# The last pair's sums, splits and stores written into the second feed-forward product's first unit, and a difference tile moved onto their memory

## The chip, the cores and the metric

The kernel runs on one core of one Trainium2 chip. The metric is the device time of one execution in microseconds. The core's engines work side by side, each through a queue of its own in a fixed order: PE multiplies matrices into accumulator banks, DVE and ACT do elementwise work (ACT also the conversions), SP issues the transfers between device memory and on-chip memory, POOL does almost nothing here.

## The reference

One layer of a hybrid trunk on 512 tokens of width 2048: a modulated norm, a projection that feeds a gated linear recurrence and a stick-breaking attention, an output projection, and then the part that this text is about, the gated feed-forward block:

```python
h = rms_norm(x, norm2_g[layer]) * (1.0 + sc2) + sh2
gate, up = jnp.split(h @ w_ffn_in[layer], 2, axis=-1)
x = x + g2 * ((jax.nn.silu(gate) * up) @ w_ffn_out[layer])
```

The inner width is 5632, which is 44 blocks of 128.

## The kernel before, in words

Every matrix product is made of three float products: each operand is split into a rounded part ("hi", a conversion on ACT, L231 or L1101) and the rest ("lo", a subtraction on DVE, L232 or L1102), and hi·hi, hi·lo and lo·hi are added up in the accumulator. Both feed-forward products also use a Strassen-like scheme with seven half-size products in place of eight. So operands have to be added and subtracted before they are split, and results have to be copied out of the accumulators and added up.

**First product.** A loop over f = 2 to 43 takes one pair of 128-wide gate and up blocks each. It loads two weight tiles (`wg`, `wu`), forms sums and differences of their halves on DVE (`ffS` L1133, then L1134 to L1136), splits them, and runs the seven products in the order 1, 2, 6, 7, 5, 4, 3, each 24 matmuls, into the accumulators `ffA`, `ffB` and `ffC`. In between ACT copies partial results out ("taps" a, b, c, u, L1027). DVE and ACT then make silu(gate)·up: the "act", 128 rows by 512 tokens.

`keep` puts the acts of two neighbouring f into one tile `forms` (L1081 for the even f, L1083 for the odd). The seven operand forms of the second product are sums of its quarters (`sums`, L1089 to L1093). `parts` then splits them, a range of forms at a time, and sends both halves to device memory, to be loaded again by the second product:

```python
S.copy(hi, R[:, q])                                               # L1101
V.tensor_sub(R[:, q].bitcast(F32R), R[:, q], hi.bitcast(F32))     # L1102
for i, t in enumerate((hi.bitcast(F32), R[:, q])):
    nc.sync.dma_start(opd[c][:, q, n - starts[c], i * HT:i * HT + HT], t)   # L1104
```

These five steps of a pair (two of `sums`, three of `parts`: forms 0 to 2, 3 and 4, 5 and 6) go into a list `later`, and `one_later()` takes one off after each product of the next f. The last pair has no next f, so `while later: one_later()` (L1169) takes its five steps between the two products. Its hi parts lie in `cond`, an older tile that the second product also uses for copies.

**Second product.** It runs in twelve units `u`, (chunk c of inner blocks) × (column half i); the first four units hold three blocks, the others four. In each unit the seven products run in the order 2, 1, 7, 6, 4, 5, 3 into accumulator pairs `foB`, `foA`, `foC`, `foA`, `foC`, `foA`, `foA`; `multiply` splits two weight blocks at a time (`wfo_<product>_<first block>`, and every fourth pair in a spare place that the profile calls `opsB`) and issues the matmuls. Weight differences are formed in place, and one of them, y3 − y0, in a tile `T2` of its own (in unit 0 in a slice of `yraw`). After product 1 the two `foA` banks are copied by `onto` (L1217 in the first two units, otherwise L1222 with an add) to the output tile `O`. Product 6 goes on adding in the same two banks, so it cannot begin before these copies have read them:

```python
def onto(dst, src, first):
    if first:
        with tc.high_priority(offset=2 * AHEAD):
            S.copy(dst, src)                                      # L1217
        return
```

**What sets the order.** The instructions are written in program order, and a scheduler of the framework puts them into a fixed order per engine, by priorities (`tc.high_priority` lifts a step), data dependencies and the reuse of memory. Tiles come from pools; `rp` holds `forms`, `tp` the other temporaries of the first product, and the second product's pool `zp` (`T2`, `ident2`, `O`) takes over their memory when both are closed (`tctx.close()`, L1171).

Of the kernel before, what the change touches and what calls it, by code (L numbers as in the profile page):

```python
# [10 lines left out]
F32 = mybir.dt.float32  # L11
# [6 lines left out]
P = 128  # L18
D = 2048
KT = 16  # L20
T = 512
# [5 lines left out]
CHUNKS = (3, 3, 4, 4, 4, 4)  # L27
# [102 lines left out]
def trunk(ctx, tc, a):  # L130
# [862 lines left out]
    later = hp.tile([P, 2, HALF, 2, HT], F32R, tag="hlo", name="opC")  # L993
    H.update({6: late[:, 0], 7: late[:, 1], 5: later[:, 0], 4: later[:, 1]})
    for j in range(HALF):
        V.tensor_sub(block(0, 0, j), block(0, 1, j), block(0, 0, j))
        t2 = ft.tile([P, HT], F32, tag="t", name=f"t2_{j}")
# [11 lines left out]
    xctx.close()  # L1009

    tctx = ctx.enter_context(ExitStack())
    tp = tctx.enter_context(tc.tile_pool(name="tp", bufs=2, side="right", reuse_waits="tile"))
    rp = tctx.enter_context(tc.tile_pool(name="rp", bufs=1, side="right", reuse_waits="tile"))
    opd = [dram.tile([P, 7, n, 2 * HT], F32, name=f"opd{c}") for c, n in enumerate(CHUNKS)]
    starts = [sum(CHUNKS[:c]) for c in range(len(CHUNKS))]

# [16 lines left out]
    def place(n):  # L1033
        n %= 11
        return places[0][:, n] if n < 4 else places[1][:, n - 4] if n < 7 else places[2][:, n - 7]

    def load_op(c, q):
        if c < len(CHUNKS):
            nc.sync.dma_start(place(7 * c + q)[:, 0:CHUNKS[c]].bitcast(F32),
                              opd[c][:, ORDER[q] - 1].rearrange("p n (h t) -> p n h t", h=2))  # L1040

    def load_y(u, b):
        if u == len(units):
            return
        c, i = units[u]
        n = CHUNKS[c]
        t = raw_tile([P, n, T], f"wfo{u}_{b}") if b % 2 == 0 else yraw[u > 0][:, b // 2, 0:n]
        nc.sync.dma_start(t, a["w_fo"][i, b][:, starts[c]:starts[c] + n])
        blocks[u][b] = t

    yraw = []
# [21 lines left out]
    forms = {}  # L1073
# [34 lines left out]
    later = []  # L1108

    def one_later():  # L1110
        if later:
            later.pop(0)()
# [13 lines left out]
    for f in range(2, FM):  # L1126
# [39 lines left out]
            keep(f, sg, up)  # L1166
        if rest:
            rest.pop(0)()
    while later:  # L1169
        one_later()  # L1170
    tctx.close()  # L1171


# [8 lines left out]


    zp = ctx.enter_context(tc.tile_pool(name="zp", bufs=1, side="right", reuse_waits="tile"))
    T2 = zp.tile([P, 4, T], F32, name="T2")
    ident2 = zp.tile([P, 512], F32, name="ident2")[:, 0:P]
    O = zp.tile([P, 4, D], F32, name="O")
    A = [att(f"foA{j}") for j in range(2)]
# [6 lines left out]
    def multiply(out, c, q, raw, first, u, sums):  # L1195
        n = CHUNKS[c]
        x = place(7 * c + q)
        for k0 in range(0, n, 2):
            w = min(2, n - k0)
            with tc.high_priority(offset=AHEAD):  # L1200
                for d, e, g in sums:
                    V.tensor_sub(*(t[:, k0:k0 + w] for t in (d, e, g)))
            whi, wlo = split(raw[:, k0:k0 + w], [P, w, T], f"wfo{u}_{q}_{k0}")
            for j in range(2):
                js = slice(j * P, j * P + P)
                for kk in range(w):
                    k = k0 + kk
                    flags = dict(stop=False, skip_group_check=True)
                    PE.matmul(out[j], x[:, k, 0, js], whi[:, kk], start=first and k == 0, **flags)
                    PE.matmul(out[j], x[:, k, 0, js], wlo[:, kk], start=False, **flags)  # L1210
                    flags["stop"] = k == n - 1
                    PE.matmul(out[j], x[:, k, 1, js], whi[:, kk], start=False, **flags)
# [6 lines that stand above are left out]
        t = cond[:, taps[0] % 4 * T:taps[0] % 4 * T + T]  # L1219
        taps[0] += 1  # L1220
        with tc.high_priority(offset=2 * AHEAD):
            S.copy(t, src)  # L1222
        V.tensor_add(dst, dst, t)
# [14 lines left out]
    def some_out(n):  # L1238
        for _ in range(min(n, len(outs))):
            emit_out(*outs.pop(0))  # L1240

    for u, (c, i) in enumerate(units):
        def dst(th, j, dh):
            return O[:, 2 * th + j, dh * 1024 + i * T:dh * 1024 + i * T + T]

        def ready(th, dh):
            if c == last_c:
                outs.extend((8 * dh + 4 * i + m, th) for m in range(4))

        first, final = c == 0, c == last_c  # L1250
        if final and i == 0:
            for g in range(4):
                nc.sync.dma_start(place(7 * c + 7 + g).bitcast(F32).rearrange("p n h t -> p n (h t)"), x1d[:, 4 * g:4 * g + 4])
        if u == 2:
            nc.sync.dma_start(ident2, a["cst"][:, 0])
        y = blocks[u]
        t2 = (T2 if u else yraw[0][:, 2])[:, 0:CHUNKS[c]]
        load_y(u + 1, 2)
        load_y(u + 1, 0)
        for q, p in enumerate(ORDER):  # L1260
            out = {2: B[i], 7: C, 4: C}.get(p, A)
            raw = {2: y[2], 1: y[0], 7: y[1], 6: t2, 4: y[2], 5: y[0], 3: y[3]}[p]
            sums = {7: [(y[1], y[3], y[1])], 6: [(t2, y[3], y[0])], 4: [(y[2], y[2], t2)]}.get(p, ())
            if p == 7:
                with tc.high_priority(offset=AHEAD):
                    for k0 in range(0, CHUNKS[c], 2):
                        ks = slice(k0, min(k0 + 2, CHUNKS[c]))
                        V.tensor_sub(y[0][:, ks], y[1][:, ks], y[0][:, ks])
            multiply(out, c, q, raw, p in (1, 7) or p == 2 and first, u, sums)
            if final:  # L1270
                some_out(3)
            for j in range(2):
                if p == 1:
                    onto(dst(0, j, 0), A[j], first)
                    if final:
                        V.tensor_add(dst(0, j, 0), B[i][j], dst(0, j, 0))
                elif p == 7:
                    onto(dst(1, j, 1), C[j], first)
                elif p == 6:
                    onto(dst(1, j, 0), A[j], first)  # L1280
                elif p == 4:
                    V.tensor_add(dst(1, j, 0), C[j], dst(1, j, 0))
                elif p == 5:
                    onto(dst(1, j, 1), A[j], False)
                elif p == 3:
                    if first:
                        S.copy(dst(0, j, 1), A[j])
                    else:
                        V.tensor_add(dst(0, j, 1), A[j], dst(0, j, 1))
            if p == 1:  # L1290
                ready(0, 0)
                if final:
                    slots += [t[:, h * HT:h * HT + HT] for t in B[i] for h in range(2)]
            elif p in (4, 5, 3):
                ready(*{4: (1, 0), 5: (1, 1), 3: (0, 1)}[p])
            if p == 7:
                load_y(u + 1, 1)
            if p == 3:
                load_y(u + 1, 3)
            if u == 0 and q == 6:  # L1300
                places.append(hp.tile([P, 4, 4, 2, HT], F32R, tag="hhi", name="opsC"))
            if q < 4 and i == (c == 0):
                load_op(c + 1, q)
            if i == 1 and 1 <= q < 4:
                load_op(c + 1, q + 3)
# [60 lines left out]
```

## Time and profile before

| | us |
|---|---|
| median of the three runs | 2292.98 |
| lowest, highest run | 2292.85, 2294.41 |
| the profiled execution | 2288.73 |
| its span, first to last instruction | 2286.7 |

The span has the first product's loop from about 1003 to 1837 us and the second product from there to the end. Rows of a timeline give the start in us, the duration of the row in us, engine, line, operation, names (out <- in), shape and count; in square brackets stands the idle time of the engine before the row and who ended it. Where a row stands for several instructions (x18), its duration runs to the modelled end of the last one; the next row's start says when the engine went on.

### The profile page before, as it was taken

The page shows a single profiled execution, that of the slowest core. Times are in us where ns is not written, and L with a number is a line of the kernel's source. Part 1 is how long each engine was busy: PE and PEld are TensorE (multiplying, and loading weights), DVE is VectorE, ACT ScalarE, POOL GpSimd, SP SyncE. Part 2 cuts the span into 40 slices and gives each one's busy share as a digit, 9 for nine tenths or more (in the row PEclk, how much of TensorE's full clock was granted, in tenths as well). Part 3 has the DMA queues.
Part 4 walks back from the last instruction along what each step waited for, and adds up shares of the span by engine and source line. Part 5 has one row for each costly group of instructions (what it writes and reads, how often), then busy time and mean ns, then how long its engine had stood idle before and what let it go on. Part 6 is the DMA issues. An engine that isn't in the chain of part 4 may idle for free.

```text
span 2286.7 us, 35537 instructions
## 1 busy us (share of the span) xinstructions
PE 2228.2 (97%) x14171; PEld 2025.8 (89%) x14171; DVE 1915.4 (84%) x2566; ACT 1156.0 (51%) x2015; POOL 10.0 (0%) x25
## 2 busy tenths in 40 slices
PE   7999899999999999999999999999999999999999
PEld 6899899878888878899999999999999977778787
DVE  8887779899887865599999888888888878888888
ACT  4326666566655522565454545455555445544443
POOL 0000000000000000000000000000000000000000
PEclk9999999999999999999999999999999999999999
DMA  9886546853332386346555644444444586666452
GB/s 369 314 326 220 174 145 228 303 188 111 112 110 74 111 310 228 97 143 226 185 208 198 225 149 169 150 153 166 132 171 143 178 310 225 238 221 221 151 199 75
DMA packets 114977, 437.68 MB, mean 191 GB/s; under 512 B 9822, under 2 KB 58236, under 8 KB 76796
## 3 DMA queue, kind: packets, MB, share of 16 engines
q1 hardware_dynamic: 114812, 435.42, 53.1%
q8 instruction: 111, 1.82, 0.3%
q14 instruction: 54, 0.44, 0.1%
HBM read 386.61 MB, written 48.77 MB: 190 GB/s over the span
## 4 chain that ended last, share of the span: by engine, by line
PE 64%; DVE 20%; DMA 7%; issue 5%; ACT 3%; SPq 0%; DVEq 0%; ACTq 0%
PE ffA L93 10%; PE foA L93 9%; PE wo L93 7%; PE sbp L93 7%; PE ffC L93 5%; PE foC L93 4%; PE st L93 4%; PE hgf L93 3%; PE hgg L93 3%; PE hgq L93 3%; DVE ff L232 3%; DMA opd<-fhi 2%; PE ffB L93 2%; PE ff L93 2%; DVE ada L179 1%
## 5 line engine op out<-in xcount | busy, mean ns | idle before, releaser
L93 PE MATMUL sbp<-wsb,hhi 128*128 128x384 f32 x1024 | 269.8, 343 | 3.1 <-DVE wsb L232 1.7
L179 DVE SCALAR_TENSOR_TENSOR ada<-ada,cond 128x2048 f32<-128x2048 f32 x95 | 217.0, 2289 | 48.1 <-DMA ada<-in_w_ada 47.9
L93 PEld LDWEIGHTS sbp<-wsb,hhi 128*128 128x128 f32 x1024 | 185.2, 190 | 7.9 <-issue 3.3
L93 PE MATMUL sbp<-wsb,hlo 128*128 128x384 f32 x512 | 172.9, 338 | 0.0
L93 PE MATMUL wo<-ohi,wo 128*128 128x512 f32 x480 | 150.2, 392 | 4.1 <-ACT wo L231 1.6
L232 DVE TENSOR_TENSOR wfo<-wfo,wfo 128x1024 fp32r<-128x1024 f32 (+1 forms) x72 | 83.3, 1164 | 39.7 <-ACT wfo L231 39.3
L93 PEld LDWEIGHTS wo<-ohi,wo 128*128 128x128 f32 x480 | 89.7, 188 | 24.3 <-ACT wo L231 2.9
L93 PE MATMUL ffA<-opD,ff 128*128 128x256 f32 x768 | 99.0, 286 | 4.0 <-ACT u L1027 4.0
L231 ACT CAST wfo<-wfo 128x1024 fp32r<-128x1024 f32 (+1 forms) x72 | 72.2, 1007 | 60.1 <-PE foA L93 56.9
L93 PE MATMUL ffC<-opC,ff 128*128 128x256 f32 x768 | 94.7, 279 | 5.8 <-ACT c L1027 5.8
L93 PEld LDWEIGHTS ffA<-opD,ff 128*128 128x128 f32 x768 | 95.6, 194 | 4.5 <-ACT u L1027 4.5
L1101 ACT CAST fhi<-forms 128x512 fp32r<-128x512 f32 (+1 forms) x63 | 43.7, 693 | 109.3 <-DMA opd<-fhi 76.2
L93 PEld LDWEIGHTS sbp<-wsb,hlo 128*128 128x128 f32 x512 | 97.0, 190 | 0.8 <-issue 0.5
L93 PEld LDWEIGHTS ffC<-opC,ff 128*128 128x128 f32 x768 | 90.8, 188 | 7.2 <-ACT c L1027 7.2
L93 PE MATMUL ffA<-opB,ff 128*128 128x256 f32 x768 | 93.3, 277 | 1.7 <-ACT ff L231 1.0
L93 PE MATMUL wo<-olo,wo 128*128 128x512 f32 x240 | 93.5, 390 | 0.1
L93 PE MATMUL ffB<-opA,ff 128*128 128x256 f32 x768 | 92.7, 276 | 0.0
L93 PEld LDWEIGHTS ffA<-opB,ff 128*128 128x128 f32 x768 | 90.1, 188 | 2.2 <-ACT ff L231 1.2
L93 PE MATMUL ffA<-opA,ff 128*128 128x256 f32 x744 | 89.9, 276 | 0.8 <-DVE ff L232 0.8
L93 PE MATMUL ffA<-opC,ff 128*128 128x256 f32 x744 | 90.1, 277 | 0.0
L93 PEld LDWEIGHTS ffB<-opA,ff 128*128 128x128 f32 x768 | 89.8, 188 | 0.0
L93 PE MATMUL ffC<-opB,ff 128*128 128x256 f32 x744 | 89.7, 276 | 0.0
(1008 smaller groups left out, 5955.5 us busy)
## 6 DMA issues: line engine op xcount, KB each, us to landing
ada<-in_w_ada SPq DMA_DIRECT2D x95, 1024.0 KB, 5.2
wfo<-in_w_fo SPq DMA_DIRECT2D x16, 1024.0 KB, 5.7
yraw<-in_w_fo SPq DMA_DIRECT2D x16, 1024.0 KB, 4.9
fix<-in_w_fix SPq DMA_DIRECT2D x14, 1024.0 KB, 5.5
opd<-forms SPq DMA_DIRECT2D x44, 256.0 KB, 4.7
opd<-fhi SPq DMA_DIRECT2D x42, 256.0 KB, 4.4
opsC<-opd SPq DMA_DIRECT2D x10, 1024.0 KB, 4.8
opsA<-opd SPq DMA_DIRECT2D x9, 1024.0 KB, 7.0
```

The lines of the kernel that those rows point to most:

```text
L93: self.engine.matmul(out, lhsT, rhs, **kw)
L179: V.scalar_tensor_tensor(w, w, 1.0, row, op0=ALU.mult, op1=ALU.mult, accum_out=col)
L231: S.copy(hi, r)
L232: V.tensor_sub(lo, r, hi.bitcast(F32))
L1101: S.copy(hi, R[:, q])
```

## The change

Three things are edited. The steps of the last pair are no longer taken in a row between the products; unit 0 of the second product takes two of them after its second product (q = 1, product 1), two after the third (product 7) and one after the fourth (product 6). For that the tile `forms` has to live on: its pool `rp` is opened ahead of `tp` and stays open. And `T2` is no longer a tile of `zp`, but the next tile of the tag `forms` in `rp`, allocated at u = 1, so that it lies where the forms of the last pair lay.

```diff
     tctx = ctx.enter_context(ExitStack())
+    rp = ctx.enter_context(tc.tile_pool(name="rp", bufs=1, side="right", reuse_waits="tile"))
     tp = tctx.enter_context(tc.tile_pool(name="tp", bufs=2, side="right", reuse_waits="tile"))
-    rp = tctx.enter_context(tc.tile_pool(name="rp", bufs=1, side="right", reuse_waits="tile"))
...
         if rest:
             rest.pop(0)()
-    while later:
-        one_later()
     tctx.close()
...
     zp = ctx.enter_context(tc.tile_pool(name="zp", bufs=1, side="right", reuse_waits="tile"))
-    T2 = zp.tile([P, 4, T], F32, name="T2")
+    T2 = []
...
         y = blocks[u]
-        t2 = (T2 if u else yraw[0][:, 2])[:, 0:CHUNKS[c]]
+        if u == 1:
+            T2.append(rp.tile([P, 4, T], F32, tag="forms", name="T2", bufs=1))
+        t2 = (T2[0] if u else yraw[0][:, 2])[:, 0:CHUNKS[c]]
...
             elif p in (4, 5, 3):
                 ready(*{4: (1, 0), 5: (1, 1), 3: (0, 1)}[p])
+            for _ in range({1: 2, 2: 2, 3: 1}.get(q, 0) if u == 0 else 0):
+                one_later()
             if p == 7:
                 load_y(u + 1, 1)
```

The built programs show where the scheduler puts the instructions. The first place is ACT in unit 0, from the conversion for product 6's first two weight blocks (`wfo_3_0`) on. `CAST cond<-forms` are the last pair's conversions, `COPY O<-foA` the two copies after product 1, `COPY O<-foC` those after product 7; the numbers behind a name are allocation numbers and differ between the builds. Before:

```order
L231 CAST wfo_3_0_18442<-yraw_18316 128x1024
L231 CAST opsB<-yraw_18316 128x512
L231 CAST wfo_3_2_18458<-yraw_18316 128x512
L231 CAST wfo_4_0_18470<-wfo_2_18311 128x1024
L1101 CAST cond<-forms_18089 128x512
L231 CAST opsB<-wfo_2_18311 128x512
L1101 CAST cond<-forms_18089 128x512
L1101 CAST cond<-forms_18089 128x768
L1217 COPY O<-foA_18351 128x512
L1217 COPY O<-foA_18352 128x512
L1217 COPY O<-foC 128x512 x2
```

The same place with the change:

```order
L231 CAST wfo_3_0_18436<-yraw_18316 128x1024
L1215 COPY O<-foA_18333 128x512
L1215 COPY O<-foA_18334 128x512
L231 CAST opsB<-yraw_18316 128x512
L231 CAST wfo_3_2_18452<-yraw_18316 128x512
L231 CAST wfo_4_0_18468<-wfo_2_18311 128x1024
L1101 CAST cond<-forms_18089 128x512
L1215 COPY O<-foC 128x512 x2
L231 CAST opsB<-wfo_2_18311 128x512
L1101 CAST cond<-forms_18089 128x768
L1101 CAST cond<-forms_18089 128x512
```

The conversions of the last pair stood in unit 0 already; what moved is the copies of `foA`, from behind seven conversions to the place right behind `wfo_3_0`, and with them the copies of `foC`.

The second place is DVE in the same stretch, where the lo parts are made and the forms summed (`L1202`/`L1200`: weight differences). Before:

```order
L1202 TENSOR_TENSOR wfo_2_18311<-wfo_2_18311,yraw_18316 128x1024
L232 TENSOR_TENSOR opsB<-yraw_18316,opsB 128x512
L232 TENSOR_TENSOR wfo_3_0_18442<-yraw_18316,wfo_3_0_18442 128x1024
L232 TENSOR_TENSOR wfo_3_2_18458<-yraw_18316,wfo_3_2_18458 128x512
L1202 TENSOR_TENSOR wfo_2_18311<-wfo_2_18311,yraw_18316 128x512
L1089 TENSOR_TENSOR forms_18089<-forms_18089 128x256
```

With the change:

```order
L1200 TENSOR_TENSOR wfo_2_18311<-wfo_2_18311,yraw_18316 128x1024
L232 TENSOR_TENSOR wfo_3_0_18436<-yraw_18316,wfo_3_0_18436 128x1024
L232 TENSOR_TENSOR opsB<-yraw_18316,opsB 128x512
L232 TENSOR_TENSOR wfo_3_2_18452<-yraw_18316,wfo_3_2_18452 128x512
L1200 TENSOR_TENSOR wfo_2_18311<-wfo_2_18311,yraw_18316 128x512
L1089 TENSOR_TENSOR forms_18089<-forms_18089 128x256
```

The lo part of product 7's third block (`opsB<-yraw`) now stands behind that of product 6's first two (`wfo_3_0`).

The third place is DVE at the start of the first product's loop, f = 2, where the two pools' exchanged places in memory change what a first write waits for. Before:

```order
L1081 TENSOR_TENSOR forms_8651<-held 128x2x256
L1133 TENSOR_TENSOR ffS_8658<-wu2r 128x1024
L1083 TENSOR_TENSOR forms_8651<-held 128x2x256
L1134 TENSOR_TENSOR wu2r<-wg2r,wu2r 128x1024
L1089 TENSOR_TENSOR forms_8651<-forms_8651 128x256
L1135 TENSOR_TENSOR wg2r<-ffS_8658,wg2r 128x1024
L232 TENSOR_TENSOR ff_7lo_8761<-wu2r,ff_7hi_8760 128x1024
```

With the change:

```order
L1133 TENSOR_TENSOR ffS_8658<-wu2r 128x1024
L1081 TENSOR_TENSOR forms_8651<-held 128x2x256
L1134 TENSOR_TENSOR wu2r<-wg2r,wu2r 128x1024
L1083 TENSOR_TENSOR forms_8651<-held 128x2x256
L1135 TENSOR_TENSOR wg2r<-ffS_8658,wg2r 128x1024
L232 TENSOR_TENSOR ff_7lo_8761<-wu2r,ff_7hi_8760 128x1024
L1136 TENSOR_TENSOR wg2r<-wg2r 128x1024
```

The weight sums moved ahead of two multiplications and one sum of the acts. From here to f = 8 some rows of DVE, ACT and SP change places with neighbours; from there to the last f the orders are the same, and they differ again only in units 0 and 1 of the second product (on SP in the transfers that are issued then). The order on PE is the same throughout.

## The prediction

> **What bounds the kernel now.** I read the page first, then the waits of PE, then the timelines where its longest wait of the second product lies.
>
> ```profile
> PE 2228.2 (97%) x14171; PEld 2025.8 (89%) x14171; DVE 1915.4 (84%) x2566; ACT 1156.0 (51%) x2015; POOL 10.0 (0%) x25
> ...
> PE ffC L93 <- ACT c L1027: 6.1, 7, 1.6
> ...
> PE foA L93 <- ACT O L1217: 3.7, 1, 3.7
> ```
>
> PE is busy for 97% of the span, so only what PE waits for, or runs slowly through, is to be had. The last row is one wait of 3.7 us for the copies of `foA` into `O`, and the change moves just these. Here is PE around it, then the clock that it was granted (windows with the busy time of PE, PEld, DVE, ACT and POOL, the granted clock, the DMA share and GB/s).
>
> ```profile
> 1840.95 4.24 PE L93 MATMUL foA<-wfo,opsA 128*128 128x512 f32 x18
> 1845.03 2.88 PE L93 MATMUL foC<-wfo,opsA 128*128 128x512 f32 x12
> 1847.75 1.52 PE L93 MATMUL foC<-opsB,opsA 128*128 128x512 f32 x6
> 1852.98 5.97 PE L93 MATMUL foA<-wfo,opsA 128*128 128x512 f32 x18 [3.71 <-ACT O L1217]
> 1858.78 2.88 PE L93 MATMUL foC<-wfo,opsB 128*128 128x512 f32 x12
> ...
> 1849.00:1853.00 4.00, 0.29 (x3) 0.03 (x1) 4.00 (x8) 3.19 (x7) 0.00 (x0) 1.00 0.20 69
> 1853.00:1859.00 6.00, 6.00 (x19) 4.78 (x20) 0.94 (x2) 2.77 (x5) 0.00 (x0) 0.72 0.92 280
> ```
>
> Product 1 (18 matmuls) goes from 1840.95 to 1845.03, 4.08 us. Product 6, the same 18, goes from 1852.98 to 1858.78, 5.80 us: after the wait the clock was 0.72 over 6 us, and a loss of 6 × 0.28 = 1.68 us fits the difference of 1.72. The wait thus costs PE 3.71 + 1.72 = 5.43 us.
>
> Why the copies were late is seen on ACT (first fence) and DVE (second):
>
> ```profile
> 1843.91 1.06 ACT L231 CAST wfo<-yraw 128x1024 fp32r<-128x1024 f32 x1 [2.10 <-PE foA L93]
> 1844.87 0.61 ACT L231 CAST opsB<-yraw 128x512 fp32r<-128x512 f32 x1
> 1845.39 0.61 ACT L231 CAST wfo<-yraw 128x512 fp32r<-128x512 f32 x1
> 1847.99 1.05 ACT L231 CAST wfo<-wfo 128x1024 fp32r<-128x1024 f32 x1 [1.99 <-PE foC L93]
> 1849.12 0.62 ACT L1101 CAST cond<-forms 128x512 fp32r<-128x512 f32 x1
> ...
> 1850.67 0.62 ACT L1101 CAST cond<-forms 128x512 fp32r<-128x512 f32 x1 [0.42 <-DVE forms L1090]
> 1851.61 0.83 ACT L1101 CAST cond<-forms 128x768 fp32r<-128x768 f32 x1 [0.32 <-DVE forms L1093]
> 1852.35 1.06 ACT L1217 COPY O<-foA 128x512 f32<-128x512 f32 x2
> 1853.30 1.09 ACT L1217 COPY O<-foC 128x512 f32<-128x512 f32 x2
> ```
>
> ```profile
> 1838.17 0.68 DVE L1083 TENSOR_TENSOR forms<-sg,up 128x512 f32<-128x512 f32 x1
> ...
> 1844.59 1.22 DVE L1202 TENSOR_TENSOR wfo<-wfo,yraw 128x1024 f32<-128x1024 f32 x1
> 1845.72 0.69 DVE L232 TENSOR_TENSOR opsB<-yraw,opsB 128x512 fp32r<-128x512 f32 x1
> 1848.66 0.42 DVE L1089 TENSOR_TENSOR forms<-forms 128x256 f32<-128x256 f32 x1
> ```
>
> The copies had their data when product 1 ended, at about 1845.2, and ran at 1852.35, in order behind conversions that wait for DVE's sums of the forms (0.42 and 0.32 us) and for PE (1.99). The steps of the last pair ran inside unit 0 already, so the change's words describe no move of theirs; what it alters is the place of the copies in ACT's row.
>
> **The change part by part: the copies.** With ACT's new order I lay the durations above in a row. `wfo_3_0` is converted from 1843.91 on; at 1844.87 the first `foA` bank is complete (it ends three matmuls of 4.08 / 18 = 0.227 us ahead of product 1), the second at about 1845.2. The two copies take 0.95 (1852.35 to 1853.30), to 1845.82. Then `opsB` (0.52, from 1844.87 to 1845.39) ends at 1846.34, `wfo_3_2` at 1846.86, and `wfo_4_0` still waits for PE until 1847.99. PE asks for product 6 at 1849.11 (1847.75 and six matmuls of 0.227): the copies have then been done for 3.3 us, and the wait goes. What is late next is the row that was pushed back. `opsB` is needed by product 7's third block, hi at 1847.75 and lo one matmul later, at 1847.98. Hi is there at 1846.4. Lo is made on DVE, now behind `wfo_3_0`'s: 1845.72 + 1.13 (from 1844.59 to 1845.72, a subtraction of 1024 columns) = 1846.85, + 0.69 = 1847.54. That is 0.44 us early, the tightest cover in the change; beyond it every us is a us of PE.
>
> The copies of `foC` come behind the first `cond` conversion: that waits for L1089 (ends 1849.08), so 1849.1 to 1849.6, copies to 1850.6. Product 4 needs them at 1849.11 + 4.08 = 1853.19. The remaining rows of ACT (`opsB` 0.52, `cond` 0.74 and 0.52) end near 1852.4, `wfo_5_0` at 1853.3, its lo at 1854.8; product 5 begins at 1857.3. So nothing in unit 0 keeps PE, and I take the whole 5.43 us. The ends: nothing of it, if another wait takes the place of this one, and 5.43.
>
> **The last pair's sums, splits and stores** are as many instructions as before on DVE and ACT, in the same unit. SP sends the same six transfers; behind them in its queue stands unit 1's load of y3:
>
> ```profile
> 1849.76 0.38 SPq L1104 DMA_DIRECT2D opd<-cond  x1
> 1854.65 1.02 SPq L1104 DMA_DIRECT2D opd<-forms  x1
> 1855.72 1.83 SPq L1048 DMA_DIRECT2D yraw<-in_w_fo  x1
> ...
> yraw<-in_w_fo SPq DMA_DIRECT2D x4, 768.0 KB, 5.5
> ...
> 1874.99 1.82 DVE L1202 TENSOR_TENSOR yraw<-yraw 128x1024 f32<-128x1024 f32 x2
> ```
>
> The first store waits for the `cond` conversion, which is done near 1849.6 as before; the last conversion ends near 1852.4 and the last lo part by 1853.7 (two of 0.69 or less behind it), so the last store and y3's load go out about 1 us earlier than at 1854.65 and 1855.72. The load takes some 5.5 us to land (a median of four), so y3 lies there near 1861; DVE first uses it at 1874.99, and with PE 5.4 us ahead at about 1869.5. Cost nothing, cover 8 us. `cond` is overwritten by copies after product 5, near 1861; its stores were issued by 1852.5. `T2` on the forms' memory must wait until the stores have read it; DVE's first write to it comes right behind those two subtractions, past 1871, some 10 us after. `ident2`'s load goes later in SP's queue, ahead of weights for unit 2. Cost nothing, each.
>
> **The exchanged pools at f = 2.** DVE and PE there:
>
> ```profile
> 1007.34 0.69 DVE L1081 TENSOR_TENSOR forms<-held 128x512 f32<-128x512 f32 x1
> 1007.94 1.23 DVE L1133 TENSOR_TENSOR ffS<-wu2r 128x1024 f32<-128x1024 f32 x1
> 1009.07 0.69 DVE L1083 TENSOR_TENSOR forms<-held 128x512 f32<-128x512 f32 x1
> 1009.67 1.23 DVE L1134 TENSOR_TENSOR wu2r<-wg2r,wu2r 128x1024 f32<-128x1024 f32 x1
> 1011.14 1.23 DVE L1135 TENSOR_TENSOR wg2r<-ffS,wg2r 128x1024 f32<-128x1024 f32 x1
> ...
> 1012.03 0.51 PE L93 MATMUL ffC<-opB,ff_7hi 128*128 128x256 f32 x2 [2.01 <-ACT ff_7hi L231]
> 1013.50 0.79 PE L93 MATMUL ffA<-opB,ff 128*128 128x256 f32 x2 [0.96 <-ACT ff L231]
> 1101.35 3.09 PE L93 MATMUL ffC<-opC,ff 128*128 128x256 f32 x24 [0.69 <-ACT c L1027]
> 1145.93 4.63 PE L93 MATMUL ffA<-opD,ff 128*128 128x256 f32 x24 [2.10 <-ACT u L1027]
> 1657.17 3.10 PE L93 MATMUL ffC<-opC,ff 128*128 128x256 f32 x24 [1.57 <-ACT c L1027]
> ...
> 1012.00:1018.00 6.00, 5.00 (x27) 4.80 (x28) 6.00 (x7) 2.94 (x3) 0.00 (x0) 0.72 0.30 126
> 1145.00:1151.00 6.00, 5.07 (x30) 5.07 (x31) 5.01 (x7) 2.87 (x4) 0.00 (x0) 0.72 0.95 373
> ```
>
> PE waits twice for DVE's chain. In the new order L1134 starts at 1007.34 + 1.13 + 0.60 = 1009.07, 0.60 earlier, and L1135 at 1010.81, 0.33 earlier. The first wait (2.01) shrinks by 0.60, but the second (0.96) hangs on L1135, so PE comes out 0.33 us ahead. DVE runs without a gap there, so the moved multiplications delay later rows by no more than they freed. From f = 3 to 8 neighbours swap on three queues; PE's only wait in that stretch is the 0.69 at 1101.35. I can't follow each swap, so I bound them: the gain is at most all of 2.01 + 0.96 + 0.69 and the clock loss behind the first (1.68 again), 5.34; the loss is one wait as long as the stretch's worst neighbour, 2.10 with the same 1.68, 3.78. I take −0.33, the row that I can work out, as the others rest on conversions and taps in unchanged numbers.
>
> **The sum.** 5.43 + 0.33 = 5.76 us less. The profiled execution took 2288.73 us (span 2286.7 and 2.0 around it), so it would take 2282.97. The median of the runs, 2292.98, lies 4.25 above it, a difference that I can't place, and I carry the gain over unchanged: 2287.2 us. About 0.2%, 4.6 us, is what a measurement of this kernel tells from no change.
>
> **The clock, and a rule.** Three waits, of 2.01 (with 0.96 soon behind), 2.10 and 3.71 us, are each followed by 6 us at 0.72; a wait of 1.57 at 1657.17 is not (24 matmuls in 3.10 us, as behind the 0.69). [...]
>
> **The rivals.**
> - *A rest of the wait stays*, because `opsB`'s parts come after product 7 asks for them, or the copies wait for something that the trace of before hides. For it: 0.44 us of cover. Against it: every term is a measured duration. With a rest of 2.10 the gain is 1.65 + 0.33, 2291.0 us.
> - *The gain is taken back later*: unit 1 or 2 then waits for an operand. For it: the DMA share is 0.92 behind the wait. Against it: 8 us of cover at y3, and loads are issued when buffers come free, which moves ahead too. Only the 0.33 is left: 2292.65.
> - *The change doesn't do what its place suggests*: `O` lies on memory of the closed pool `tp`, and the copies wait for its last users whatever their place, so PE waits as before. Against it: those are the taps and act halves, last read by DVE at 1838.17 to 1838.85, and a store of `fhi` from inside the first product. 2292.65 too.
> - *Slower: the swapped rows at f = 3 to 8.* On ACT the conversions of `fhi` wait for the store that last read that tile, and where one stands ahead of a tap, PE waits for the tap, as at 1145.93: 2.10 + 1.68 = 3.78 us. Six units have new orders. Two such waits about cancel the gain; from the third on the kernel is slower: 3 × 3.78 − 5.76 = +5.6, 2298.6 us. Against it: PE waits in this stretch but once, for 0.69, and the taps keep their order.
>
> [...]
>
> **How the numbers follow.** The forecast 0.78, a rest of the wait 0.06, taken back 0.04, not done 0.05, the slower one 0.07. Of the forecast's 0.78, 0.65 falls beyond 4.6 us of gain, as 5.76 is 1.2 past it and the clock and the scatter of the runs (1.6 us among three) can eat that; 0.13 falls within. The three middle rivals (0.15) and 0.03 of the slower one are no change, 0.04 is slower. Faster 0.65, same 0.31, slower 0.04. The range runs from both terms at their best, 2292.98 − 5.43 − 5.34 = 2282.2, to the forecast with one wait of 3.78 new in the first product, 2292.98 − 5.43 + 3.78 = 2291.3; it holds the rest of the wait too. The other three rivals, 0.16, stay out.
>
> **What would show it.** On PE the row of 18 `foA` matmuls of product 6 begins right behind the six of `opsB`, without a bracket, and lasts 4.2 us, with a clock of 1.00. On ACT the copies of `foA` stand behind `wfo_3_0`. At f = 2 the waits are about 1.4 and 1 us. Wrong it would be by a new wait of `foC<-opsB` for DVE, by PE waiting in unit 1 for a load, or by new waits for taps between 1020 and 1130.

## The result, and the profile after

| | before | after |
|---|---|---|
| median of the runs, us | 2292.91 (2289.72 to 2295.95, 6 runs) | 2285.69 (2281.46 to 2286.49, 6 runs) |
| profiled execution, us (span) | 2288.73 (2286.7) | 2285.77 (2283.9) |
| first `ffA` matmul to first `foB` matmul (first product), us | 833.73 | 835.76 |
| first `foB` matmul to the end (second product), us | 449.91 | 444.22 |

The ratio is 0.9966, with a 95% interval of 0.9955 to 0.9977: 5.3 to 10.3 us less, and 7.2 between the medians. The kernel is faster; the forecast of 2287.2 us is 1.5 us above the median and the time lies inside the range.

The two profiled executions differ by only 3.0 us. The table says why: the second product became 5.69 us shorter, the first was 2.03 us longer in this execution, and it began 0.81 us later, behind code that is the same in both. The runs below show how much the first product differs by itself.

The place on which the forecast rests is PE in unit 0, here in the timeline of after, and in windows of it (busy time of PE, PEld, DVE, ACT and POOL, granted clock, DMA share, GB/s):

```profile
1847.88 2.88 PE L93 MATMUL foC<-wfo,opsA 128*128 128x512 f32 x12
1850.60 1.52 PE L93 MATMUL foC<-opsB,opsA 128*128 128x512 f32 x6
1851.95 4.24 PE L93 MATMUL foA<-wfo,opsA 128*128 128x512 f32 x18
1856.04 2.88 PE L93 MATMUL foC<-wfo,opsB 128*128 128x512 f32 x12
```

```profile
1849.00:1853.00 4.00, 4.00 (x19) 3.33 (x18) 4.00 (x6) 2.90 (x6) 0.00 (x0) 1.00 0.40 158
1851.00:1857.00 6.00, 6.00 (x28) 4.95 (x28) 5.97 (x10) 5.93 (x10) 0.00 (x0) 1.00 0.36 117
```

Product 6 (18 matmuls) has no bracket any more: it starts 1.35 us after the six matmuls on `opsB` (1850.60 to 1851.95), where it was 5.23 us (1847.75 to 1852.98), and it runs at clock 1.00, from 1851.95 to 1856.04, 4.09 us in place of 5.80. That is 3.88 + 1.71 = 5.59 us of the 5.69. ACT and the DVE row that was pushed back:

```profile
1846.76 1.06 ACT L231 CAST wfo<-yraw 128x1024 fp32r<-128x1024 f32 x1 [2.10 <-PE foA L93]
1847.72 1.06 ACT L1215 COPY O<-foA 128x512 f32<-128x512 f32 x2
1848.67 0.63 ACT L231 CAST opsB<-yraw 128x512 fp32r<-128x512 f32 x1
...
1849.71 0.68 DVE L232 TENSOR_TENSOR opsB<-yraw,opsB 128x512 fp32r<-128x512 f32 x1
...
1851.96 0.62 ACT L1101 CAST cond<-forms 128x512 fp32r<-128x512 f32 x1
1852.49 1.06 ACT L1215 COPY O<-foC 128x512 f32<-128x512 f32 x2
...
1853.98 1.35 ACT L1101 CAST cond<-forms 128x768 fp32r<-128x768 f32 x2
```

The copies of `foA` stand behind the first conversion and are done by 1848.8; product 6 asks at 1851.95. Of the waits that the second product had, the one for the copies (3.7 us) is gone. The other four read 4.0, 1.6, 1.0 and 0.3 us in before, in this order, and are what they were:

```profile
PE foC L93 <- DVE wfo L232: 4.0, 5, 1.3
PE foC L93 <- DVE opsB L232: 1.6, 3, 0.5
PE foB L98 <- DVE O L1232: 1.0, 1, 1.0
PE foC L93 <- ACT wfo L231: 0.3, 1, 0.3
```

At f = 2 the two waits of 2.01 and 0.96 have become these, with the clock still at 0.72 behind them:

```profile
1012.24 0.50 PE L93 MATMUL ffC<-opB,ff_7hi 128*128 128x256 f32 x2 [1.42 <-ACT ff_7hi L231]
1013.98 0.50 PE L93 MATMUL ffA<-opB,ff 128*128 128x256 f32 x2 [1.23 <-ACT ff L231]
```

```profile
1012.00:1018.00 6.00, 4.53 (x23) 4.32 (x24) 6.00 (x6) 3.12 (x4) 0.00 (x0) 0.72 0.47 175
```

Their sum is 2.65 in place of 2.97, 0.32 less.

### The profile page after: what moved, and what is told of

Its sections match the earlier page's. It is cut to its first block, busy times and chain, and to the rows that moved or that the text cites. A ratio compares the mean times of both kernels' runs of the same rounds, so it can differ in the third digit from the quotient of the medians.

```text
span 2283.9 us, 35536 instructions
## 1 busy us (share of the span) xinstructions
PE 2228.5 (98%) x14171; PEld 2025.3 (89%) x14171; DVE 1916.0 (84%) x2566; ACT 1155.4 (51%) x2015; POOL 10.0 (0%) x25
## 4 chain that ended last, share of the span: by engine, by line
PE 53%; DVE 24%; DMA 14%; issue 6%; ACT 4%; SPq 0%; DVEq 0%; ACTq 0%
PE foA L93 9%; PE sbp L93 8%; PE wo L93 7%; DMA opd<-fhi 5%; PE foC L93 5%; DVE ff L232 4%; PE st L93 4%; PE hgf L93 4%; PE hgg L93 3%; PE hgq L93 3%; PE ffA L93 3%; DMA ada<-in_w_ada 2%; PE ffC L93 1%; ACT fhi L1101 1%; DVE ada L179 1%
```

## The experiments

The theory was that the place of the copies of `foA` in ACT's order makes the gain, and the exchange of the pools next to nothing. The rivals were that spreading the last pair's steps over unit 0 makes it, or the reordered front. The change has four parts: the pools `rp` and `tp` change places, `rp` stays open, `T2` leaves `zp`, and the steps are spread. "Second product" below is the time from the first `foB` matmul to the end of the span, in the profiled execution of each.

| kernel | ratio to before (95%) | second product, us | product 6 waits, us | f = 2 waits, us |
|---|---|---|---|---|
| before | | 449.91 | 3.71 | 2.01, 0.96 |
| after | 0.9966 (0.9955 to 0.9977) | 444.22 | none | 1.42, 1.23 |
| after, timed again | 0.9974 (0.9966 to 0.9983) | 444.04 | none | 1.42, 1.23 |
| after, steps put back | 0.9972 (0.9961 to 0.9984) | 444.38 | none | 1.61, 1.23 |
| pools exchanged only | 1.0021 (1.0009 to 1.0032) | 457.24 | 10.1 | 1.42, 1.24 |
| `T2`'s own pool only | 0.9973 (0.9963 to 0.9982) | 444.19 | none | 2.02, 0.97 |
| both of these | 0.9966 (0.9953 to 0.9978) | 444.32 | none | 1.42, 1.23 |

**The steps put back.**

```
 # after, at the end of the first product
+    while later:
+        one_later()
     tctx.close()
```

> The kernel after, with the last pair's steps put back ahead of the end of the first product (while later: one_later() in front of tctx.close()); the exchange of the pools and the place of T2 stay as after. Theory: the gain hangs on what the copies of foA into O wait for, and with rp still open and O no longer behind the last pair's work in that pool they come ahead of the conversions without the move of the steps: 5 to 9 us below the kernel before, within 1.5 us of after's 2285.7, and in unit 0 the 18 matmuls of foA <- wfo,opsA begin right behind the six on opsB, 4.2 us at clock 1.00. Rival: it is the spreading of the steps over the second product that does it: then only the reordered front is left, 2292.6, and product 6 of unit 0 waits about 3.7 us again with the clock at 0.72 behind it.

Measured: 2285.53 us against 2291.69, and product 6 without a wait. The built program has the same order on every engine with and without these two lines. So what the change's name says first, that the steps are done during the second product's first unit, does nothing by itself: the scheduler put them there already.

**The pools exchanged, nothing else.**

```
 # before
+    rp = tctx.enter_context(tc.tile_pool(name="rp", ...))
     tp = tctx.enter_context(tc.tile_pool(name="tp", ...))
-    rp = tctx.enter_context(tc.tile_pool(name="rp", ...))
```

> The kernel before, with only the two pools exchanged inside the first product's stack (rp opened first, tp second; both closed at its end as before). Theory: this does the early part alone. The waits in f = 2 read about 1.4 and 1.2 us in place of 2.01 and 0.96 (-0.3 us), product 6 of unit 0 keeps its wait of about 3.7 us and its 6 us at 0.72: 0.3 us below the kernel before, 2292.6, with 2290.5 to 2294.5 as what runs scatter by. Rival: the early part is worth more than the rows say (a shorter first product, up to the 5.3 us of the lower bound): 2287.5 to 2289.

Measured: 2296.95 us against 2291.69, slower by 2.1 to 7.3 us. I had expected 0.3 us less, and both theories missed. The timeline shows it, and the window behind the wait:

```profile
1854.09 0.83 ACT L1101 CAST cond<-forms 128x768 fp32r<-128x768 f32 x1 [0.32 <-DVE forms L1093]
1861.21 1.07 ACT L1217 COPY O<-foA 128x512 f32<-128x512 f32 x2 [6.29 <-DMA opd<-forms]
...
1861.85 6.88 PE L93 MATMUL foA<-wfo,opsA 128*128 128x512 f32 x18 [10.10 <-ACT O L1217]
...
1868.57 2.90 PE L93 MATMUL foC<-wfo,opsB 128*128 128x512 f32 x12
```

```profile
1862.00:1868.00 6.00, 6.00 (x16) 4.70 (x17) 0.00 (x0) 1.89 (x4) 0.00 (x0) 0.56 0.47 184
```

With the places of the closed pools exchanged, `O` lies on the bytes of `forms`, and the first copy into it waits for the stores that read them, 6.29 us on ACT and 10.10 on PE, and then runs at 0.56. By starts, as above: product 6 comes 11.62 us behind the matmuls on `opsB` (1850.23), 10.27 more than in after, and takes 6.72 in place of 4.09, 2.63 more; together 12.9, and the second product is 13.0 longer than after's. The third rival of the prediction, copies that wait for the last users of a closed pool's bytes, is what happens here. In after it does not, because `rp` is still open and `O` lies on `tp`'s bytes alone.

**`T2` in a pool of its own, nothing else.** In before, `zp` held `T2` and `O`; `T2` lay on `forms`, `O` on `tp`'s bytes. This is worked out from the tiles' sizes and not read from addresses: in each of the 128 rows of on-chip memory `forms` and `T2` take 8 KiB each, `tp`'s tiles 34 and `ident2` with `O` 34, and the run above shows on which side `O` lies. So the change did not bring `T2` onto other bytes than before; it took it out of `O`'s pool. Here only the pool is split:

```
 # before
-    T2 = zp.tile([P, 4, T], F32, name="T2")
     ident2 = zp.tile([P, 512], F32, name="ident2")[:, 0:P]
     O = zp.tile([P, 4, D], F32, name="O")
+    t2p = ctx.enter_context(tc.tile_pool(name="t2p", bufs=1, side="right", ...))
+    T2 = t2p.tile([P, 4, T], F32, name="T2")
```

> The kernel before with one thing changed: T2 gets a pool of its own, opened behind zp, so that the pool of O no longer reaches over the bytes of forms. The order of every engine up to the second product is that of before, row for row; behind it the copies of foA stand ahead of the conversions as in after. This is the late part alone. Theory (the copies' place in ACT's order is the gain): product 6 of unit 0 begins right behind the matmuls on opsB, no wait of 3.7 us, clock 1.00; the second product lasts 444 to 445 us in place of 449.9; 4.5 to 8 us below the kernel before. Rival (the gain comes from the reordered front): within 2 us of before.

Measured: 2284.49 us against 2291.01, 4.1 to 8.5 us less. This is the late part alone, with before's order in all of the first product:

```profile
1846.26 1.07 ACT L1218 COPY O<-foA 128x512 f32<-128x512 f32 x2
...
1849.14 1.52 PE L93 MATMUL foC<-opsB,opsA 128*128 128x512 f32 x6
1850.50 4.24 PE L93 MATMUL foA<-wfo,opsA 128*128 128x512 f32 x18
1850.51 0.62 ACT L1101 CAST cond<-forms 128x512 fp32r<-128x512 f32 x1
...
1011.26 0.50 PE L93 MATMUL ffC<-opB,ff_7hi 128*128 128x256 f32 x2 [2.02 <-ACT ff_7hi L231]
1012.74 0.50 PE L93 MATMUL ffA<-opB,ff 128*128 128x256 f32 x2 [0.97 <-ACT ff L231]
```

The waits at f = 2 are those of before, product 6 waits for nothing, and the second product is as short as in after. So the copies were late in before because they wrote into a pool of which another tile lay on `forms`: the scheduler set all of the pool's users behind the last pair's steps. That last step is read from the six builds of the table (late in the two where `T2` is in `zp`, early in the four others), not from a run. Of the two late ones only before bears it out by itself, as with the pools exchanged `O` lies on `forms` directly.

**Both edits, still without the rest of the change.**

```
 # before, with rp opened ahead of tp, and
+    t2p = ctx.enter_context(tc.tile_pool(name="t2p", bufs=1, side="right", ...))
+    T2 = t2p.tile([P, 4, T], F32, name="T2")
     zp = ctx.enter_context(tc.tile_pool(name="zp", ...))
-    T2 = zp.tile([P, 4, T], F32, name="T2")
```

> The run with only the pools exchanged, and T2 in a pool of its own opened ahead of zp; the steps of the last pair stay in front of the end of the first product and forms' pool closes there. Every engine's order is that of after, row for row. Theory: if the order is all that matters, 5 to 9 us below before and the same second product as after, 444 to 445 us; the copies wait for no store, where with the exchange alone they waited 6.3 us on ACT for the stores of forms (10.1 us of PE). Rival (closing the pool costs something by itself): a wait in front of product 6 or a second product above 446 us.

Measured: 2282.17 us against 2291.01; a second product of 444.32 us. Every engine has after's order, so closing `rp` costs nothing in itself.

**After, timed again.**

> The kernel after, unchanged, timed beside the next run on one chip, for a second sample of it: 5.5 to 8 us below before, a second product of 444.2 to 444.7 us, and a first product anywhere from 833.7 to 836 us, since that is what the runs of equal orders gave so far. If the 7.2 us measured first held a real share of the reordered front beyond the 0.3 us of its rows, the time stays 1.5 us or more below the kernel with T2's own pool alone (which was 6.2 us below before); if that was scatter, it falls within 1.5 us of it.

Measured: 2285.08 us against 2291.00, 5.9 less; the first product took 836.08 us and the second 444.04, each just outside its expected range. With the exchange the four ratios are 0.9966, 0.9974, 0.9972 and 0.9966, without it 0.9973. The early term is not larger than these intervals let one see, which fits 0.3 us and does not prove it. In the profiled executions the first product took 833.73 and 835.88 us with the order of before (before, and `T2`'s own pool only) and between 832.88 and 837.32 in seven with that of after (the rest of the table and the two runs that follow); the 2.03 us that the profiled execution of after lost there are within this.

**Longer copies.** To see how much cover the copies have, the copy of one bank, then of both, was made four times as long:

```
 # after, onto(), unit 0, product 1
-                S.copy(dst, src)
+                S.copy(<four pieces of O's row>, <src, four times>)
```

> The kernel after; product 1's copy of the first foA bank in unit 0 writes its four T-wide pieces of O's row (four times the bank, later overwritten), so product 6 can begin only when a copy that is about 1.6 us longer ends. The copies ended 3.3 us ahead of product 6 and the conversions behind them on ACT gave 0.44 us of cover at product 7's third block. Theory of the cover: beyond 0.44 us every us of delay on ACT is a us of PE, a wait of about 0.6 to 1.2 us in front of the last matmuls on opsB, clock 1.00 there and no more lost: 0.6 to 1.2 us above after. Rival: the slack is larger than the row says (the wait for opsB's second half is not on ACT's chain): no wait at all, time as after.

> As the run before, with both banks' copies four times as long: some 3.2 us more on ACT. By the rows of before (waits of 2.01 and 2.10 us were each followed by 6 us at 0.72, one of 1.57 by none) a wait of 2.0 to 2.8 us ahead of opsB's last matmuls costs itself and a further 1.7 us at clock 0.72: 3.7 to 4.5 us above after. [...]

Measured, one execution each: 2284.71 and 2285.57 us, second products of 444.65 and 444.50. Neither shows the loss expected. In the second run:

```profile
1847.18 3.63 ACT L1279 COPY O<-foA 128x2048 f32<-128x2048 f32 x2
1850.06 1.52 PE L93 MATMUL foA<-wfo,opsA 128*128 128x512 f32 x6
1850.70 0.62 ACT L231 CAST opsB<-yraw 128x512 fp32r<-128x512 f32 x1
...
1851.41 0.45 PE L93 MATMUL foC<-opsB,opsA 128*128 128x512 f32 x1
1851.71 0.63 PE L93 MATMUL foA<-wfo,opsA 128*128 128x512 f32 x2
1852.17 1.35 PE L93 MATMUL foC<-opsB,opsA 128*128 128x512 f32 x5
```

The copies took 2.57 us more (3.63 against 1.06), and the scheduler, knowing that `opsB` would come late, set eight of product 6's matmuls ahead of product 7's last five (two in the first run). At most 0.43 us (first run) and 0.28 (second) reached the end, where second products of after's order differ by up to 0.34 us among themselves. These two runs are inconclusive on the cover at a fixed order, and on the clock behind a wait of 2.0 to 2.8 us, as no wait arose.

**The first product's waits.** The scatter of the first product suggested what else could go: the high part of the forms has one buffer, `fhi`, and ACT's conversion into it waits for the store of the part before (in after 21 waits of up to 3.8 us between 1425 and 1825 us), with PE's taps queued behind. Two edits were tried. The first lets the pairs from f = 21 on use `cond`, which has a place for each part:

```
 # after, parts(): cond in place of fhi
-            if f < FM - 1:
+            if f < 21:
```

> The kernel after, where from f = 21 on the high parts of the forms go into cond in place of the one fhi buffer (up to then only the last f did so), so that ACT's conversion no longer waits for the store of the part before. After f = 21 the kernel after shows 2.7 us of PE waiting for taps behind such conversions (1.6 once for c, 1.1 in three for b). Theory: the first product's waits come from these stores, so 1.5 to 4 us below after. Rival (the taps wait for something else, or the time comes back at the next tap): within 1 us of after.

The second kernel has the first one's edit in it as well, and beside it two buffers and smaller pieces, which act without it only before f = 21:

```
 # after: cond from f = 21 on; before that two buffers of two forms; four pieces
-            if f < FM - 1:
+            if f < 21:
-    hi = tp.tile(..., tag="fhi", name=f"fhi{f}_{a}", bufs=1)
+    hi = tp.tile(..., tag="fhi", name=f"fhi{f}_{a}", bufs=2)
-    later.extend([..., partial(parts, 0, 3), partial(parts, 3, 5), partial(parts, 5, 7)])
+    later.extend([..., partial(parts, 0, 2), partial(parts, 2, 4), partial(parts, 4, 6), partial(parts, 6, 7)])
```

> The kernel after with two buffers of fhi, of two forms each, in place of one of three, and the parts cut into four pieces (0-2, 2-4, 4-6, 6-7) in place of three: a conversion waits for the store of the part before the last. The kernel after shows 11.9 us of PE waiting for the taps a, b, c and u in the first product, and the lengths of that product differ by 3 us between runs of the same order. Theory: most of these waits stand behind fhi conversions that wait for a store: 5 to 12 us below after, and the spread of the single runs becomes smaller. Rival: one more conversion, difference and pair of stores for each f (0.5 us more of ACT) uses the gain up: within 2 us of after, or above it.

Measured: 2275.40 us (ratio 0.9936, 0.9924 to 0.9949) and 2277.95 us (0.9944, 0.9930 to 0.9958). Both beat both kernels: some 7 and 5 us below after, by the ratios. The first gains more than I expected, the second lies at the lower edge of its 5 to 12. PE from 1425 to 1825 us, in after and then in the first of the two:

```profile
1425.00:1825.00 400.00, 397.19 (x3439) 395.81 (x3438) 336.28 (x381) 202.08 (x296) 0.00 (x0) 1.00 0.46 157
```

```profile
1425.00:1825.00 400.00, 400.00 (x3502) 400.00 (x3501) 337.65 (x381) 207.56 (x302) 0.00 (x0) 1.00 0.45 159
```

The first column behind the length is PE, with its matmuls. It does 63 more in the same 400 us, at 400 / 3502 = 0.114 us each 7.2 us. In after the lists of waits of PE and of ACT for the same stretch name 2.7 us on PE, with ACT waiting for `fhi`'s stores:

```profile
PE ffC L93 <- ACT c L1027: 1.6, 1, 1.6
PE ffA L93 <- ACT b L1027: 1.1, 3, 0.6
```

```profile
ACT fhi L1101 <- DMA opd<-fhi: 45.9, 21, 3.8
```

All three rows are gone in both variants, which have the same edit there. My expectation took the listed waits for the whole; the other 4.5 us are in none of them. The count of matmuls shows them, and so does the time from one f to the next (first `ffB` matmul to first `ffB` matmul): from f = 21 to f = 43 it adds up to 430.77 us in after and to 422.40 in both variants, 19.20 for every f.

The two buffers and the four pieces gained nothing where they stood alone. From f = 2 to f = 21, counted in the same way, after took 384.61 us, the first variant 384.10 and the second 384.14. ACT's waits for the stores did become shorter there (19.5 us in place of 31.0, from 1015 to 1395 us), but PE did not come out ahead. So the gain of both kernels is that of `cond` from f = 21 on, and the theory that two buffers would remove most waits fails. That the stores are what was in the way is read from the waits that went; the edit also moves rows of DVE and ACT, and the two were not separated. The spread of the single runs did not become clearly smaller (3.7 and 4.8 us, against 5.0 and 5.8 for after).

**The two gains without the exchange.**

```
 # before, with T2 in its own pool behind zp, and in parts()
-            if f < FM - 1:
+            if f < 21:
```

> The kernel before with two edits: T2 in a pool of its own behind zp, and the high parts of the forms in cond from f = 21 on. No exchange of pools, no deferral. Theory: the two gains lie in different places and add up: 6.2 us from the copies and the 7 us that the second edit took out behind f = 21 (all pairs there at 19.20 us): 12 to 15 us below before, and level with the kernel after with cond from f = 21 (15 us below) to within 2 us. Rival (the exchange or the deferral is needed for the rest): 10 us below before or less.

Measured: 2279.27 us against 2291.00 (0.9953, 0.9941 to 0.9965), 11.7 between the medians. That is just short of the 12 to 15 expected. The interval, 8.0 to 13.5 us, reaches into the expectation and into the rival's 10 or less, so this run does not decide between them. PE is busy for all of 1425 to 1825 here too. The 4 us between this kernel and after with `cond` from f = 21 are more than the 2 expected. Whether they are the exchange or scatter stays open: the intervals overlap, and the profiled executions took 2277.16 and 2276.84 us.

## Why the prediction was right, point by point

- *The copies, 5.43 us.* Right in mechanism and size: the second product became 5.69 us shorter, and with only this part changed the kernel gained 4.1 to 8.5 us. The wait was a little more than its bracket says: from start to start it was 3.88 us, as the bracket counts from the modelled end of the row before, which reaches 0.17 us past the next start (1.52 against 1.35).
- *The cover at product 7's third block, 0.44 us.* The lo part ended at 1849.71 + 0.68 = 1850.39; PE asked for it one matmul behind 1850.60, at 1850.83: 0.44 us early. That beyond it every us is a us of PE did not show in the runs with longer copies, where the order on PE changed too; at a fixed order it was not tried.
- *The cover of the stores and of y3.* The stores and the load behind them went out later than I worked out: the load at 1858.45, 18.8 us behind the first `foB` matmul (1839.69), where before it was 18.9 (1855.72 against 1836.84); I had about 1 us less. It cost nothing:

```profile
1857.73 0.67 SPq L1104 DMA_DIRECT2D opd<-forms  x1
1858.45 0.70 SPq L1048 DMA_DIRECT2D yraw<-in_w_fo  x1
...
1872.24 1.82 DVE L1200 TENSOR_TENSOR yraw<-yraw 128x1024 f32<-128x1024 f32 x2
```

  From issue to use are 13.8 us; with the 5.5 us of the landing, 8.3 us of cover, as said.
- *f = 2, 0.33 us.* The waits show 0.32. The bound of −5.34 to +3.78 for the rest of the front was far too wide for what came; in after no tap wait of 3.78 us arose at f = 3 to 8 (the slower rival). It is not ruled out by the order, though: in one execution with the same order there, the first run with longer copies, PE waited 3.24 us for the tap u at 1148.06, with the clock at 0.74 behind it, where before had its 2.10 and after 0.99 (at 1145.55). How long such a wait is differs from one execution to the next, and what the exchange is worth over the whole first product is below what these runs tell apart.
- *The sum against the profiled execution.* 2282.97 was forecast and 2285.77 came: 2.8 us more, all of it in front of the second product, where the orders that the terms rest on were right but an execution differs by 2 to 3 us from the next. The prediction carried the gain to the median unchanged, and there it holds.
- *Which part of the change does it.* The prediction said that the words of the change describe no move of the last pair's steps. The run with the steps put back shows it.

## What to carry to other kernels

A tile that shares a pool with another one can be held back by what lies under the other: split a pool that is opened on a closed pool's bytes by what each tile must wait for, and look where each tile comes to lie before two pools change places, since that alone cost 10.1 us of waiting here. Search for the one instruction that PE waits for and ask why it stands where it does in its engine's row, and not only what it reads. Where many small waits are suspected, count the instructions of the engine in a window against a run without the suspect: 63 matmuls told of 7.2 us, of which the list of waits had 2.7.

## What the runs showed of the chip

In these executions the clock did not follow the length of a wait alone. The kernel with both edits has after's order, and at f = 2 the same waits of 1.42 and 1.23 us; after them after ran at 0.72 (above), and this one did not:

```profile
1012.00:1018.00 6.00, 4.52 (x36) 4.31 (x37) 6.00 (x6) 3.15 (x4) 0.00 (x0) 1.00 0.48 178
```

Later in the same execution a wait of 2.14 us (at 1194.20) cost no clock and one of 1.79 (at 1227.31) did:

```profile
1194.00:1200.00 6.00, 5.80 (x49) 5.80 (x50) 6.00 (x8) 2.73 (x5) 0.00 (x0) 1.00 0.04 12
1227.00:1233.00 6.00, 5.69 (x35) 5.69 (x36) 5.18 (x7) 2.89 (x5) 0.00 (x0) 0.72 0.97 366
```

Over the twelve profiled executions, between f = 3 and the end, none of 53 waits of 0.9 to 1.73 us in the first product was followed by a lower clock, four of eight of 1.75 to 2.14 us were (0.72 over the 6 us behind each), and all three of 3.24, 3.71 and 10.1 us (0.74, 0.72 and 0.56 over the 6 us behind them). At 0.72 the loss is 6 × 0.28 = 1.68 us. Two waits of 1.76 us had different ends: the clock was 0.72 behind the one at 1198.17 in the run with both copies longer, and 1.00 behind the one at 1226.03 in after with `cond` from f = 21.

What differed is where a wait fell. In the trace of before the clock was at 0.50 three times in the two products, from 1013.44, 1146.56 and 1853.12 us on, for 3.41 us each; these starts are 133.12 and 706.56 us apart, 39 and 207 times 3.413 us. Here are stretches of this length, counted from a start at 0.50 in the same execution, two of after and then six of the kernel with both edits:

```profile
1010.96:1014.37 3.41, 0.90 (x5) 0.69 (x6) 3.41 (x5) 2.54 (x3) 0.00 (x0) 1.00 0.42 132
1014.37:1017.78 3.41, 3.41 (x18) 3.41 (x18) 3.41 (x4) 1.45 (x2) 0.00 (x0) 0.50 0.42 175
```

```profile
1009.03:1012.44 3.41, 1.99 (x17) 1.79 (x16) 3.41 (x5) 1.04 (x1) 0.00 (x0) 1.00 0.00 0
1012.44:1015.85 3.41, 2.18 (x17) 1.97 (x17) 3.41 (x4) 2.94 (x3) 0.00 (x0) 1.00 0.82 308
1189.94:1193.35 3.41, 2.12 (x19) 1.92 (x17) 1.49 (x3) 2.26 (x4) 0.00 (x0) 1.00 0.50 179
1193.35:1196.76 3.41, 2.56 (x21) 2.56 (x22) 3.41 (x5) 1.75 (x3) 0.00 (x0) 1.00 0.26 89
1224.07:1227.48 3.41, 1.61 (x14) 1.41 (x13) 2.81 (x3) 1.11 (x3) 0.00 (x0) 1.00 1.08 398
1227.48:1230.89 3.41, 3.41 (x17) 3.41 (x18) 2.65 (x3) 0.93 (x2) 0.00 (x0) 0.50 1.02 372
```

In after both waits at f = 2 fall into one stretch: PE is busy for 0.90 us of it and idle for 2.51, and the next stretch runs at 0.50. With both edits an edge lies between the two waits (1.42 and 1.23 us idle), and the clock stays at 1.00. The wait of 2.14 us is cut by an edge as well (1.29 and 0.85 us), the one of 1.79 is not. Of all such stretches at full clock between 1000 and 2260 us in before and after, the four in which PE was idle for 2.10, 2.51, 2.90 and 3.27 us were each followed by one at 0.50, and of 727 with 1.57 us or less none. This is what went together in these traces; no run moved a wait against the edges.

The edges lie differently in these executions (at f = 2 one is at 1013.44 us in before, at 1014.37 in after and at 1012.44 with both edits), so whether a wait of 1.8 to 2.1 us costs its 1.7 us could not be told beforehand. The prediction takes such a loss as certain behind a rest of 2.10 us (5.43 − 2.10 − 1.68 = 1.65, in the first rival). That a wait of 2.0 us or more is followed by a loss, as I took it from three rows, is wrong in that range: behind the one of 2.14 us there was none.
